# A fourth buffer for the high parts of expert weights, in place of one raw buffer

## The chip, the cores and the metric

The kernel runs on one core of one Trainium2 chip. The metric is the device time of one execution in microseconds (us). The median of three runs of the kernel before is 1669.49 us (1668.41 to 1675.79). A profiled execution took 1665.06 us; its span, from the first to the last instruction, is 1663.4 us.

## What is computed

A trunk of two layers works on 256 tokens of width 1024 in float32. Layer 0 is a mixer (gated positions and an attention with forgetting), a cross-attention to 256 memory tokens, and a dense SwiGLU of width 2816. Layer 1 is a second mixer (differential attention and a short convolution), another cross-attention, and a router that sends each token to 2 of 8 SwiGLU experts of width 3584. A norm ends it. This case is about the experts:

```python
def swiglu(h, wg, wu, wd):
    return (jax.nn.silu(h @ wg) * (h @ wu)) @ wd

def moe_swiglu(h, w_router, wg, wu, wd):
...
    logits = (t @ w_router).astype(jnp.float32)
    top_v, top_i = lax.top_k(logits, TOP_K)
    gates = jax.nn.softmax(top_v, axis=-1)
    combine = jnp.sum(jax.nn.one_hot(top_i, N_EXPERTS, dtype=jnp.float32) * gates[..., None], axis=1)
    for e in range(N_EXPERTS):
        out = out + combine[:, e:e + 1].astype(t.dtype) * swiglu(t, wg[e], wu[e], wd[e])
```

The three weight matrices of an expert are 1024 x 3584, 1024 x 3584 and 3584 x 1024 floats, 42 pieces of 1 MiB; the eight experts have 336.

## The kernel before

Every weight goes the same way, in pieces of 1 MiB (128 partitions x 2048 floats). A load on the sync engine's DMA queue (SP) brings it into a **raw** buffer. ACT copies it in two halves into a tile `wh` of a shorter float format (the high part, L121). DVE subtracts, `wl = raw - wh` (the low part, L123), and is the last to read the raw buffer. TensorE (PE) then multiplies: activations are split in the same way into `ch` and `cl`, or `hs` with its two halves, and a product is the sum of high x high (L138), low x high (L141) and high x low (L144). `mm3` issues the products with `wh` first, eight matmuls of a piece, and the four with `wl` behind them. So `wh` comes free earlier than `wl`. For the experts at the places 2, 4 and 7 (`SMALL`, at most 64 tokens) both parts of the activations stand side by side in the 128 columns, and `mm2` (L994) does with eight matmuls, four with `wh` and four with `wl`.

```python
    def pick(kind):
        lst = pools[kind]
        p = lst[cnt[kind] % len(lst)]
        cnt[kind] += 1
        return p
...
    def load_w(src, a, b, parts=1):
        r = load_raw(src, a, b, parts)
        p = pick("w")
        wh = p.tile([P, a, b], F32R, tag="wh", name="wh")
        wl = p.tile([P, a, b], F32R, tag="wl", name="wl")
```

Buffers come from pools in a fixed rotation. `wp` has three buffers for `wh` and three for `wl`. For the experts the raw rotation is written out as a list of eleven places (L1094): one of `rawp`, five that the earlier layers used for activations, `RAW2` = 3 of a pool `raw2`, one more of those activations (`V`), one of `rawp`. Each buffer is reused when its last reader is done; a load waits for that on the DMA queue.

An expert runs in four chunks of its 3584 columns (1024, 1024, 1024, 512). `gate_up` (L997) takes the chunk's pieces of the gate and the up matrix, `gated` (L1020) evicts the sums: on ACT `sg` (L1030, Silu; for the small experts `sgs`, L1026), on DVE the product (L1031). `to_hT` transposes on PE into `htp` and splits on ACT and DVE into `hs` (L129, L130). `down` (L1063) multiplies the chunk before by its down pieces into `y`. Once an expert, `slots_T` (`setp`, `st`), `gather_pair` (`xg`, `ch`), `slot_rstd` (`rsp`) and `scatter` (`y`, `sc`, `x`) stand between. All of these wait in the same in-order queues as the weight copies and subtractions. The order on each engine is made by the tile scheduler when the kernel is built, from the order of the code, the free buffers and the few `behind(...)` places that are written by hand; it is fixed in the program.

Before the last chunk of the last expert, `final_gain` (L1114) takes two places of the raw rotation: `gfrow`, read by two matmuls, and `gf`, the final norm's gain on all partitions, which is read by the last instructions of the program (`finish`, L1180).

```python
            p, tag = pick("raw")
            row = p.tile([1, D], F32, tag=tag, name="gfrow")
...
            p, tag = pick("raw")
            gf = p.tile([P, D], F32, tag=tag, name="gf")
```

Ten pieces follow it: four of gate and up, four down pieces of the chunk before, and two down pieces of the last chunk (L1202), which alone are loaded and split in two parts of 512 KB. Then `finish` scatters, norms and stores the output.

Of the kernel before, what the change touches and what calls it, by code (L numbers as in the profile page):

```python
# [12 lines left out]
F32R = mybir.dt.float32r  # L13
# [7 lines left out]
P = 128  # L21
# [6 lines left out]
DFF = 2816  # L28
DFFE = 3584
NE = 8  # L30
RAW2 = 3
WSPLIT = ((0, 0, 4), (1, 0, 4), (0, 4, 8), (1, 4, 8))
WSPLIT_MOE = ((0, 0, 4), (0, 4, 8), (1, 0, 8))
CHUNKS = ((0, 1024), (1024, 1024), (2048, 1024), (3072, 512))
# [21 lines left out]
def trunk_kernel(ctx: ExitStack, tc: tile.TileContext, io, out, stop=None):  # L56
# [6 lines left out]
    wp = ctx.enter_context(tc.tile_pool(name="wsplit", bufs=3))  # L63
# [17 lines left out]
    pools = {"raw": [(rawp, "raw")], "w": [wp], "split": WSPLIT}  # L81
# [12 lines left out]
# [6 lines that stand above are left out]
    def load_raw(src, a, b, parts=1):  # L100
        p, tag = pick("raw")
        r = p.tile([P, a, b], F32, tag=tag, name="raw")
        m = a // parts
        for i in range(parts):
            with behind(*gate):
                chain["dma"] = nc.sync.dma_start(r[:, i * m:(i + 1) * m, :], src[:, i * m:(i + 1) * m, :])
            gate.clear()
        return r

    def load_w(src, a, b, parts=1):  # L110
        r = load_raw(src, a, b, parts)
        p = pick("w")
        wh = p.tile([P, a, b], F32R, tag="wh", name="wh")
        wl = p.tile([P, a, b], F32R, tag="wl", name="wl")
        rf, hf, lf = (v.rearrange("p a b -> p (a b)") for v in (r, wh, wl))
        n = a * b // parts
        for part in range(parts):
            for i, c0, c1 in pools["split"]:
                sl = slice(part * n + c0 * n // 8, part * n + c1 * n // 8)
                if i == 0:  # L120
                    chain["wh"] = nc.scalar.activation(hf[:, sl], rf[:, sl], AF.Copy)  # L121
                elif i == 1:
                    chain["wl"] = nc.vector.tensor_sub(lf[:, sl], rf[:, sl], hf[:, sl].bitcast(F32))  # L123
                else:
                    nc.gpsimd.tensor_sub(lf[:, sl], rf[:, sl], hf[:, sl].bitcast(F32))
        return wh, wl
# [39 lines left out]
    def out_proj(cat, w, order, hook=None):  # L166
        ch, cl = cat
        acc = [[accp.tile([P, 512], F32, tag="acc", name="acc") for _ in range(2)] for _ in range(2)]
        def step(i, t, w2):
            wh, wl = w2  # L170
            for n in range(2):
                mm3([(acc[t][n], ch[:, order[i] * 2 + k, t * P:(t + 1) * P], cl[:, order[i] * 2 + k, t * P:(t + 1) * P],
                      wh[:, k, n * 512:(n + 1) * 512], wl[:, k, n * 512:(n + 1) * 512])
                     for k in range(2)], False, i == 0, i == 3)

        def piece(i):
            return load_w(w[order[i] * 256:(order[i] + 1) * 256, :].rearrange("(k p) n -> p k n", p=P), 2, D)

        for i in range(2):
            w2 = piece(i)  # L180
            for t in range(2):
                step(i, t, w2)
        last = [piece(2), piece(3)]
        for t in range(2):
            for i in range(2):
                step(2 + i, t, last[i])
            if hook is not None:
                hook(t, acc)
        return acc
# [50 lines left out]
    with ExitStack() as pre:  # L240
# [48 lines left out]
        def proj_ws(act, w, ncols, c0, into=None):  # L289

            ah, al = act
            wh, wl = load_w(w[:, c0:c0 + 256].rearrange("(k p) n -> p k n", p=P), KT, 256)
            ps = mmp.tile([P, 2, S], F32, tag="mm", name="pws") if into is None else into
            for f in range(2):
                o = ps[:, f, :]
                mm3([(o, wh[:, k, f * P:(f + 1) * P], wl[:, k, f * P:(f + 1) * P], ah[:, k, :], al[:, k, :])
                     for k in range(KT)], True, True, True)
            return ps

        def proj_ts(act, w, c0):  # L300

            ah, al = act
            pss = [accp.tile([P, 512], F32, tag="acc", name="pts") for _ in range(2)]
            for half in range(2):
                wh, wl = load_w(w[half * 512:(half + 1) * 512, c0:c0 + 512].rearrange("(k p) n -> p k n", p=P), 4, 512)
                for t in range(2):
                    mm3([(pss[t], ah[:, half * 4 + k, t * P:(t + 1) * P], al[:, half * 4 + k, t * P:(t + 1) * P],
                          wh[:, k, :], wl[:, k, :]) for k in range(4)], False, half == 0, half == 1)
            return pss
# [463 lines left out]
    with ExitStack() as moe:  # L773
        mA = moe.enter_context(tc.tile_pool(name="macts", bufs=1))
        sm = moe.enter_context(tc.tile_pool(name="msmall", bufs=2))
        m2 = moe.enter_context(tc.tile_pool(name="macts2", bufs=2))
        raw2 = moe.enter_context(tc.tile_pool(name="raw2", bufs=RAW2))

        def mbank(shape, name="mm"):
            return trp.tile(shape, F32, tag="tr", name=name)  # L780
# [311 lines left out]
        if done(4):  # L1092
            return
        pools["raw"] = ([(rawp, "raw")] + [(pA, tag) for tag in ("mh", "ml", "nh", "nl", "K")]  # L1094
                        + [(raw2, "raw")] * RAW2 + [(pA, "V"), (rawp, "raw")])
        cnt["raw"] = cnt["w"] = 0
        pools["split"] = WSPLIT_MOE
        xg_all = [catp.tile([P, 2, KT, P], F32R, tag=tg, name=tg) for tg in ("ch", "cl")]
        xg = xg_of(1)
# [209 lines left out]
```

## Time and profile before

| | |
|---|---|
| median of 3 runs | 1669.49 us (1668.41 to 1675.79) |
| profiled execution | 1665.06 us |
| its span, first to last instruction | 1663.4 us |
| mean granted TensorE clock | 0.992 of full speed |
| loads of expert weights | 112 + 112 + 110 of 1 MiB, 4 of 512 KB |
| HBM traffic | 461.90 MB read, 279 GB/s over the span |

In the profile, a group of instructions is named by its line, its engine and what it writes and reads (`wl<-raw,wh`); buffer numbers are left out. PE is the matmul engine, PEld its weight loads, SP the queue that issues the loads. A wait reads "who waited <- what ended the wait". The chain that ended last is followed back from the last instruction. The layers before the experts take the first 640 us or so; the experts run to about 1647 us.

### The profile page before, as it was taken

How to read it: one execution, taken by the hardware profiler on the slowest of the kernel's cores; microseconds unless marked ns; L12 is line 12 of the kernel's file. 1: busy time of each engine (PE TensorE's matmuls, PEld its weight loads, DVE VectorE, ACT ScalarE, POOL GpSimd, SP SyncE). 2: the span in 40 equal slices, each digit the busy share in tenths (PEclk: the TensorE clock that was granted, in tenths of full speed). 3: DMA queues.
4: the chain of work that ended last, by engine and by line, in shares of the span. 5: the costliest groups of instructions: out<-in, count | busy, mean ns of one | idle time of the engine just before them, and what ended most of it. 6: DMA issues, size and time to landing. Idle time of an engine off the chain costs nothing. (4 is left out here: it accounts for less than half of the span.)

```text
span 1663.4 us, 22408 instructions
## 1 busy us (share of the span) xinstructions
PE 1572.4 (95%) x8448; PEld 1310.2 (79%) x8448; DVE 1262.8 (76%) x1214; ACT 1074.4 (65%) x1396; POOL 47.1 (3%) x75
## 2 busy tenths in 40 slices
PE   8999999999999999999999889999889999999885
PEld 7799889999989887888887667777667777777653
DVE  6785655445576657899988988978888978988876
ACT  6555554344554446787777787767777767677775
POOL 1010010000000102000000000000000000000000
PEclk9999999999999999999999999999999999999998
DMA  7456466565535586899999999999999999999980
GB/s 237 163 178 214 145 217 201 177 200 180 191 127 178 187 333 245 322 341 354 360 369 361 345 358 339 338 338 375 345 363 345 340 337 347 329 351 345 358 309 28
DMA packets 175409, 464.50 MB, mean 279 GB/s; under 512 B 9074, under 2 KB 64390, under 8 KB 175164
## 3 DMA queue, kind: packets, MB, share of 16 engines
q1 hardware_dynamic: 174412, 459.80, 77.0%
q0 software_dynamic: 880, 3.19, 0.6%
q8 instruction: 68, 1.11, 0.3%
q14 instruction: 49, 0.40, 0.1%
HBM read 461.90 MB, written 2.11 MB: 279 GB/s over the span
## 5 line engine op out<-in xcount | busy, mean ns | idle before, releaser
L123 DVE TENSOR_TENSOR wl<-raw,wh 128x2048 fp32r<-128x2048 f32 (+1 forms) x527 | 983.0, 1894 | 238.0 <-ACT wh L121 235.7
L121 ACT ACTIVATE wh<-raw 128x1024 fp32r<-128x1024 f32 x866 | 852.7, 1049 | 277.1 <-PE pws L141 92.0
L138 PE MATMUL gu<-wh,ch 128*128 128x512 f32 x560 | 221.3, 396 | 2.8 <-ACT sg L1030 2.8
L141 PE MATMUL gu<-wh,cl 128*128 128x512 f32 x560 | 219.7, 393 | 0.0
L144 PE MATMUL gu<-wl,ch 128*128 128x512 f32 x560 | 152.8, 395 | 10.6 <-DVE wl L123 10.5
L138 PE MATMUL pws<-nh,wh 128*128 128x256 f32 x560 | 137.5, 283 | 0.0
L141 PE MATMUL pws<-nl,wh 128*128 128x256 f32 x560 | 137.4, 283 | 0.0
L144 PEld LDWEIGHTS gu<-wl,ch 128*128 128x128 f32 x560 | 103.5, 188 | 40.3 <-DVE wl L123 19.1
L138 PEld LDWEIGHTS gu<-wh,ch 128*128 128x128 f32 x560 | 105.5, 188 | 27.1 <-ACT sg L1030 2.9
L994 PE MATMUL gu<-wl,ch 128*128 128x512 f32 x336 | 99.8, 419 | 24.5 <-DVE wl L123 23.5
L141 PEld LDWEIGHTS gu<-wh,cl 128*128 128x128 f32 x560 | 105.6, 189 | 21.8 <-DVE cl L1111 0.4
L141 PE MATMUL y<-wh,hs 128*128 128x512 f32 x280 | 110.9, 396 | 0.0
L138 PE MATMUL y<-wh,hs 128*128 128x512 f32 x280 | 110.4, 394 | 0.0
L138 PEld LDWEIGHTS pws<-nh,wh 128*128 128x128 f32 x560 | 106.2, 190 | 1.3 <-ACT wh L121 0.9
L141 PEld LDWEIGHTS pws<-nl,wh 128*128 128x128 f32 x560 | 106.0, 189 | 0.4
L994 PEld LDWEIGHTS gu<-wl,ch 128*128 128x128 f32 x336 | 59.0, 191 | 55.1 <-DVE wl L123 45.9
L994 PE MATMUL gu<-wh,ch 128*128 128x512 f32 x336 | 97.7, 405 | 4.4 <-ACT wh L121 4.3
L138 PE MATMUL acc<-wh,ch 128*128 128x512 f32 x216 | 84.7, 392 | 0.0
L141 PE MATMUL acc<-wh,cl 128*128 128x512 f32 x216 | 84.4, 391 | 0.0
L994 PEld LDWEIGHTS gu<-wh,ch 128*128 128x128 f32 x336 | 63.3, 192 | 24.1 <-ACT wh L121 10.8
L144 PE MATMUL y<-wl,hs 128*128 128x512 f32 x280 | 79.1, 404 | 2.0 <-DVE wl L123 2.0
L144 PE MATMUL pws<-nh,wl 128*128 128x256 f32 x560 | 78.9, 283 | 0.0
(363 smaller groups left out, 2182.2 us busy)
## 6 DMA issues: line engine op xcount, KB each, us to landing
raw<-in_moe_w_up_dram SPq DMA_DIRECT2D x112, 1024.0 KB, 6.5
raw<-in_moe_w_gate_dram SPq DMA_DIRECT2D x112, 1024.0 KB, 6.4
raw<-in_moe_w_down_dram SPq DMA_DIRECT2D x110, 1024.0 KB, 6.2
raw<-in_mem_w_kv_dram SPq DMA_DIRECT2D x16, 1024.0 KB, 5.5
raw<-in_odd_w_in_dram SPq DMA_DIRECT2D x12, 1024.0 KB, 5.3
raw<-in_ffn_w_gate_dram SPq DMA_DIRECT2D x11, 1024.0 KB, 5.1
raw<-in_ffn_w_up_dram SPq DMA_DIRECT2D x11, 1024.0 KB, 5.2
raw<-in_ffn_w_down_dram SPq DMA_DIRECT2D x11, 1024.0 KB, 4.7
```

Of the source, the lines that this page charges most:

```text
L121: chain["wh"] = nc.scalar.activation(hf[:, sl], rf[:, sl], AF.Copy)
L123: chain["wl"] = nc.vector.tensor_sub(lf[:, sl], rf[:, sl], hf[:, sl].bitcast(F32))
L138: mm = nc.tensor.matmul(ps, ah, bh, start=f, stop=False, skip_group_check=bank)
L141: nc.tensor.matmul(ps, *((ah, bl) if w_left else (al, bh)), start=False, stop=False, skip_group_check=bank)
L144: mm = nc.tensor.matmul(ps, *((al, bh) if w_left else (ah, bl)), start=False, stop=e, skip_group_check=bank)
L994: mm = nc.tensor.matmul(ps, a, b[which], start=f, stop=e)
```

## The change

The list of pools for the split pieces gets a fourth entry, a new pool `wp2` of one buffer, for `wh` alone: every fourth `wh` lies there. `wl` always comes from `wp` and keeps its three buffers. The memory, 8 KiB a partition, is that of one `raw2` buffer: `RAW2` is 2, and the raw rotation has ten places. The layers before the experts are as they were.

```diff
-RAW2 = 3
+RAW2 = 2
...
         wh = p.tile([P, a, b], F32R, tag="wh", name="wh")
-        wl = p.tile([P, a, b], F32R, tag="wl", name="wl")
+        wl = wp.tile([P, a, b], F32R, tag="wl", name="wl")
...
         raw2 = moe.enter_context(tc.tile_pool(name="raw2", bufs=RAW2))
+        wp2 = moe.enter_context(tc.tile_pool(name="wsplit2", bufs=1))
...
         cnt["raw"] = cnt["w"] = 0
+        pools["w"] = [wp] * 3 + [wp2]
         pools["split"] = WSPLIT_MOE
```

The scheduler's order changes in places. The first is ACT, expert 0, where the first evictions `sg` and the first `hs` stand. Before:

```order
L121 ACTIVATE wh_6325<-raw_6323 128x1024 x2
L121 ACTIVATE wh_6344<-raw_6342 128x1024 x2
L1030 ACT_TABLE_LOAD
L1030 ACTIVATE sg_6279<-gu_6136,rs_6277 128x512
L1030 ACTIVATE sg_6279<-gu_6137,rs_6277 128x512
L129 ACTIVATE hs_6286<-htp_6287 128x512
L129 ACTIVATE hs_6294<-htp_6295 128x512
L121 ACTIVATE wh_6363<-raw_6361 128x1024 x2
```

Now, with all numbers three higher and lines from L778 on one or two further:

```order
L121 ACTIVATE wh_6328<-raw_6326 128x1024 x2
L121 ACTIVATE wh_6347<-raw_6345 128x1024 x2
L121 ACTIVATE wh_6366<-raw_6364 128x1024 x2
L1031 ACT_TABLE_LOAD
L1031 ACTIVATE sg_6282<-gu_6139,rs_6280 128x512
L1031 ACTIVATE sg_6282<-gu_6140,rs_6280 128x512
L129 ACTIVATE hs_6289<-htp_6290 128x512
L129 ACTIVATE hs_6297<-htp_6298 128x512
```

The copies of one more piece (6363, now 6366) stand ahead of `sg` and `hs`. About ten groups of `sg`, `hs` and `ch` in experts 0 and 1 have moved so by one piece on ACT, with their partners on DVE. From the second pieces of expert 2 on, ACT, DVE and PE have the same order in both kernels, but for a few matmuls of the last piece.

The second place is the DMA queue, at the loads behind `final_gain` (the names in brackets are the engines or DMA lanes whose semaphore a load waits for). Before, the last six rows of loads:

```order
L106 DMA raw_13424<-in_moe_w_down_dram 128x2x1024 [waits DMAHW2_49,DVE_49]
L106 DMA raw_13439<-in_moe_w_down_dram 128x2x1024 [waits DMAHW3_49,DVE_49]
L106 DMA raw_13469<-in_moe_w_down_dram 128x1024 [waits DMAHW4_49,DVE_49]
L106 DMA raw_13469<-in_moe_w_down_dram 128x1024 [waits DMAHW5_49]
L106 DMA raw_13480<-in_moe_w_down_dram 128x1024 [waits DMAHW6_49,PE_49]
L106 DMA raw_13480<-in_moe_w_down_dram 128x1024 [waits DMAHW7_49]
```

Now:

```order
L106 DMA raw_13427<-in_moe_w_down_dram 128x2x1024 [waits DMAHW2_49,DVE_49]
L106 DMA raw_13442<-in_moe_w_down_dram 128x2x1024 [waits DMAHW3_49,DVE_49]
L106 DMA raw_13472<-in_moe_w_down_dram 128x1024 [waits DMAHW4_49,PE_49]
L106 DMA raw_13472<-in_moe_w_down_dram 128x1024 [waits DMAHW5_49]
L106 DMA raw_13483<-in_moe_w_down_dram 128x1024 [waits DMAHW5_49,DMAHW6_49,DMAHW4_49,DVE_49]
L106 DMA raw_13483<-in_moe_w_down_dram 128x1024 [waits DMAHW7_49]
```

Order and kind of the loads are the same. The wait for PE (the matmuls that read `gfrow`) has moved from the last piece to the one before it, and the last piece (13483) waits for the lanes 4 and 5, which load the piece before it (13472), and for DVE: both have the same place in `raw2`, since `gf` keeps the other.

## Rows read from the trace of the kernel before

**Rows 1.** The page: busy time (share) and instructions; DMA busy tenths in 40 slices.

```profile
PE 1572.4 (95%) x8448; PEld 1310.2 (79%) x8448; DVE 1262.8 (76%) x1214; ACT 1074.4 (65%) x1396; POOL 47.1 (3%) x75
DMA  7456466565535586899999999999999999999980
```

**Rows 2.** Stretches: length, busy PE PEld DVE ACT POOL, clock, DMA share, GB/s.

```profile
643.00:884.00 241.00, 238.15 (x1086) 196.24 (x1085) 216.91 (x191) 187.39 (x209) 0.00 (x0) 0.99 0.94 351
884.00:1642.00 758.00, 695.57 (x3124) 535.86 (x3122) 640.75 (x451) 561.04 (x675) 0.00 (x0) 1.00 0.92 336
```

**Rows 3.** Waits of PE, 643 to 884 us: total us, times, longest us.

```profile
PE gu L138 <- ACT sg L1030: 2.8, 1, 2.8
```

**Rows 4.** Tile raw, 884 to 1590 us, and the DMA queue's waits in it.

```profile
L123 DVE TENSOR_TENSOR wl<-raw,wh x234: 2277/2284/2294, 884.4 to 1588.0; 128x2048 fp32r<-128x2048 f32 x117
DMA to landing us min/median/max: 4.7/6.5/8.5
...
SPq L106 <- DVE wl L123: 457.4, 194, 5.6
```

**Rows 5.** Waits of ACT, 643 to 884 us; then timeline rows of ACT and PE there.

```profile
ACT wh L121 <- PE gu L141: 25.7, 39, 0.8
ACT wh L121 <- PE y L141: 15.8, 20, 1.2
...
654.77 2.01 ACT L121 ACTIVATE wh<-raw 128x1024 fp32r<-128x1024 f32 x2 [0.71 <-PE gu L141]
...
660.22 2.00 ACT L121 ACTIVATE wh<-raw 128x1024 fp32r<-128x1024 f32 x2 [0.71 <-PE gu L141]
...
766.79 1.07 PE L144 MATMUL gu<-wl,ch 128*128 128x512 f32 x4
```

**Rows 6.** Waits of ACT, DVE and PE, 884 to 1642 us.

```profile
ACT hs L129 <- PE y L144: 51.8, 14, 5.9
ACT wh L121 <- PE gu L141: 4.3, 7, 0.7
...
DVE wl L123 <- ACT wh L121: 80.4, 67, 3.9
...
PE gu L994 <- DVE wl L123: 23.5, 33, 1.6
PE y L994 <- DVE wl L123: 17.2, 24, 1.4
PE gu L144 <- DVE wl L123: 10.5, 19, 0.9
```

**Rows 7.** Timeline of ACT and DVE in expert 3: start us, us, what [idle before].

```profile
1084.88 0.38 ACT L979 ACTIVATE st<-setp 128x256 fp32r<-128x256 f32 x1 [3.82 <-PE setp L977]
...
1087.77 2.29 DVE L123 TENSOR_TENSOR wl<-raw,wh 128x2048 fp32r<-128x2048 f32 x1 [3.46 <-ACT wh L121]
```

**Rows 8.** The DMA queue at the start of the experts: a wait, and an issue.

```profile
SPq L106 <- PE rlp L812: 13.3, 1, 13.3
...
633.28 0.37 SPq L106 DMA_DIRECT2D raw<-in_moe_w_gate_dram  x1
```

**Rows 9.** Tile raw, 1613 to 1617 us, then 1600 to 1664 us.

```profile
L106 SPq DMA_DIRECT2D raw<-in_moe_w_down_dram x4: 333/339/355, 1613.9 to 1615.6; - x4
...
DMA to landing us min/median/max: 4.9/6.1/7.4
...
L121 ACT ACTIVATE wh<-raw x31: 614/1044/1067, 1599.9 to 1643.1; 128x1024 fp32r<-128x1024 f32 x23, 128x512 fp32r<-128x512 f32 x8
L123 DVE TENSOR_TENSOR wl<-raw,wh x17: 1216/2285/2293, 1599.4 to 1645.2; 128x2048 fp32r<-128x2048 f32 x13, 128x1024 fp32r<-128x1024 f32 x4
```

**Rows 10.** The chain that ended last, from 1636 us: start us, us, what.

```profile
1642.94 3.50 DVE wl L123 x3
...
1646.48 0.51 PE y L994
```

**Rows 11.** DMA issues: count, KB each, median us to landing.

```profile
x<-in_x_dram SPq DMA_DIRECT2D x2, 512.0 KB, 3.4
```

## The prediction

> **What bounds the kernel now.** I read the page first. Engine shares over the whole span tell little here, so note only that no engine is full [rows 1]: PE 95% by a busy time that counts pipelined matmuls, DVE 76%, ACT 65%, and that the DMA digits stand at 9 from the 18th slice on. From there the experts run.
>
> The stretches split the expert stage in two [rows 2]. 643 to 884 us holds experts 0 and 1, 884 to 1642 us the other six, after that comes the end. In the first stretch PE is busy 238.15 of 241 us and its only wait on another engine is 2.8 us, once [rows 3]: PE is the bound. In the second PE has 695.57 of 758 us, DVE 640.75, ACT 561.04: none is full, they hold each other up.
>
> Loads look like the limit (DMA share 0.92) but are not. 234 splits from 884.4 to 1588.0 us make 703.6 / 233 = 3.02 us a tile, and a load lands 4.7 to 8.5 us after its issue [rows 4]. The DMA queue waits 457.4 us, 194 times, for a `wl` subtraction, the last reader of a raw buffer [rows 4]: loads are late because buffers are full, not the reverse. Eleven buffers turn over in 11 x 3.02 = 33 us; less 8.5 us to land and some 9 us of splitting (two copies 2.1, one subtraction 2.3, with waits of up to 3.9 each [rows 6] counted in), a landed tile lies unused for at least 15 us.
>
> Next the waits, by stretch. Before 884 us ACT waits for PE to give back a `wh` buffer: 25.7 + 15.8 us in 59 waits [rows 5]. That is the wait the fourth buffer removes, and it stands where PE is the bound. After 884 us the same wait is 4.3 us in 7 cases. What stops ACT there is its own order: `hs`, `sgs`, `sg`, `st` and `y` stand in its queue and need a PE result, 51.8 us for `hs` alone. DVE then waits 80.4 us for `wh`, and PE 23.5 + 17.2 + 10.5 = 51.2 us for `wl` [rows 6]. One such case: at 1084.88 us ACT has idled 3.82 us for `setp`, and DVE's next subtraction idles 3.46 us behind it [rows 7].
>
> **The change, part by part.**
>
> *The fourth `wh` buffer, experts 0 and 1.* ACT starts a tile when PE has ended the high products of the third tile before; the rows repeat 2.01 us of copies after 0.71 us of waiting, 2.72 us a tile, which is PE's own pace [rows 5]. With four buffers ACT starts one tile sooner, and PE is no faster: 0 us. What DVE can gain is its lead at 884 us. Before, its subtraction begins 2.0 us (two copies) after PE ended those products; in the changed kernel it is held by the three `wl` buffers, which PE gives back four matmuls, 1.07 us, after them [rows 5]. So DVE enters expert 2 up to 1.0 us earlier. I take **-1.0 us**, since DVE limits expert 2; the bounds are 0 and, with all of the 4.3 us as well, -5.3 us.
>
> *The fourth `wh` buffer, experts 2 to 7.* The order listings of both kernels are the same on ACT, DVE and PE from early in expert 2 almost to the end; the sequence around `setp` [rows 7] stands unchanged. So ACT meets the same PE results at the same places, with fewer than three tiles in hand, and the buffer stays unused: 0 us of the 80.4.
>
> *The moved rows on ACT.* In experts 0 and 1 about ten `sg`, `hs` or `ch` groups stand one tile of copies (2.0 us) later. At the first, the copies from 660.22 us started when a buffer came free [rows 5], and `sg` stands right behind them. Now there is one buffer more: the same instant starts the copies of the next tile, `sg` stands behind these, and begins when it did: 0 us. If the cover fails, see rival 2.
>
> *One raw buffer less.* The ring shrinks by 3.0 us out of at least 15: 0 us. At the start of the stage four loads of chunk 1 change places on the DMA queue; the load that waits 13.3 us for the router's matmuls and is issued at 633.28 us is now the first of that chunk, lands by 633.3 + 8.5 = 642 us, and its copies start at 654.77 us [rows 5, 8]: 0 us.
>
> *The last load.* This is what costs. `final_gain` draws two raw buffers; its `gf` stays in one until the end. Both now come from the two-buffer pool, and so do the last two tiles. The last tile must therefore share a buffer with the one before it: in the listing its DMA waited for PE and now waits for that tile's loads and DVE. In the trace of before it is issued at about 1615.1 and 1615.6 us and is there long before its turn [rows 9]. In the changed kernel it goes out when the preceding tile's second `wl` ends. The last three of the chain's `wl` run 3.50 us from 1642.94; the first of them is that one, so it ends at 1642.94 + 3.50 / 3 = 1644.1, and the third at 1646.44 [rows 10]. The halves go out at 1644.15 and, by the spacing (1615.6 - 1613.9) / 3 = 0.57, 1644.7. How long the second takes alone is not shown: the four of its size took 4.9 to 7.4 us among others [rows 9], the quietest of 512 KB 3.4 us [rows 11]. I take 4.3, between 3.4 and 4.9, as little else moves then: 1649.0. Then two copies of 0.61 and a subtraction of 1.22 [rows 9], 2.4 us: 1651.4, against 1646.4. **+5.0 us**, bounds +4.1 (3.4 us) and +8.1 (7.4 us). Nobody hides it: that `wl` chain is the chain that ended last [rows 10], PE needs the tile for both halves of `y`, and behind it on DVE stand only `y` and what follows; on the DMA queue only the output.
>
> **Sum**: -1.0 + 5.0 = +4.0 us on the profiled execution's 1665.06, so 1669.1. That execution is 4.4 us under the median shown, 1669.49; I forecast against the median: **1673.5 us**. 0.5% is 8.3 us, about what a measurement of this kernel can tell from no change.
>
> **The rivals.**
>
> 1. *The bubbles close* (faster). The same gap stands again and again on DVE before `wl`: 80.4 us in 67 waits. If it stood for a missing buffer, a fourth could take what PE loses to it, 51.2 us; half of that, with the end's cost, gives 1669.5 - 26 + 5 = 1648. Against it: 4.3 us of buffer waits and the unchanged order. The Trainium skill's Perfetto Trace Analysis, Optimization Strategy, says that a gap repeating on an engine that should be saturated can mean that memory for the next tile ran out; the trace does not bear it out here after 884 us, and does before it, on an engine that is not the bound. Chance 0.07.
>
> 2. *The moved rows come late* (slower). If ACT has not gained a tile where `sg` or `hs` was put behind one more, PE waits 2.0 us longer for its banks or its `hs`, at ten places: up to 20 us, 1669.5 + 4 + 20 = 1693. It shows as a loss over 0.5% from three such places on (4 + 3 x 2 = 10 > 8.3). For it: PE's one wait there, 2.8 us for `sg`, is of this kind. Against it: 41.5 us of ACT's idle time there were buffer waits. Chance 0.07.
>
> 3. *The last load does not matter* (the change does nothing at the end): the wait is over early, or a shorter queue elsewhere pays for it. Then 1669.5 - 1.0 = 1668.5. Against it: the subtraction waited for is itself on the last chain. Chance 0.13.
>
> **How the numbers follow.** The forecast has 0.73. Of it 0.70 is within 0.5% and 0.03 above, for the 8.1 us bound with a slow landing. Faster by over 0.5%: 0.07, rival 1. Slower: 0.07 + 0.03 = 0.10. Within: 0.70 + 0.13 = 0.83. The range takes rival 3 and the bounds: low end 1669.5 - 5.3 + 4.1 = 1668.3, and 2 us less since the runs shown start 1.1 below their median, 1666; high end 1669.5 + 8.1 = 1677.6, and as much again, 1679. Outside lie rival 1 and most of rival 2.
>
> **What would show it.** From 884 us to about 1638, less about 1 us, all as before: DVE still waits some 80 us for `wh`, ACT some 50 us for `hs`. ACT's waits on PE for `wh` before 884 us gone. The DMA queue's last two loads not at 1615 us but some 28 us later, right behind a `wl`; then an idle DVE of about 6 us on the chain that ended last. Loads still landing in 5 to 8 us. The prediction is wrong if DVE's wait for `wh` shrinks by tens of us (rival 1), if PE waits for `sg` or `hs` before 884 us (rival 2), or if the final `wl` follows its forerunner without a gap (rival 3).

## The result, and the profile after

The changed kernel took 1679.23 us, median of 13 runs (1673.82 to 1684.78), against 1669.36 us for the kernel before in the same session (13 runs, 1663.7 to 1675.79). The ratio is 1.0058, 95% interval [1.0041, 1.0075]. Run again in another session (the experiment after_again) it took 1675.29 us against 1668.1, ratio 1.0045 [1.0032, 1.0057]. So the change costs 7 to 10 us, about half a per cent; forecast were +4.0 us, and the first median lies 0.23 us above the top of the range.

The page, busy time by engine and DMA tenths, against [rows 1]: the same numbers of instructions, PE busy 11 us longer.

```profile
PE 1583.6 (94%) x8448; PEld 1315.4 (78%) x8448; DVE 1264.0 (75%) x1214; ACT 1072.2 (64%) x1396; POOL 47.0 (3%) x75
...
DMA  7456456555545586899999999999999999999971
```

The stretches of the expert stage, the border shifted by 7 us since the layers before came out later (columns as in [rows 2]). In a stretch of the same length as before, 758 us, PE, DVE and ACT do the same work in the six later experts, at the same rate of loads.

```profile
643.00:891.00 248.00, 245.11 (x1118) 201.28 (x1118) 222.49 (x196) 189.03 (x211) 6.71 (x4) 0.99 0.94 346
891.00:1649.00 758.00, 696.04 (x3122) 535.01 (x3121) 638.37 (x449) 557.91 (x671) 0.00 (x0) 1.00 0.92 337
```

The waits of 650 to 891 us, the same work as 643 to 884 us before [rows 3, 5]. PE's one wait for `sg` is 2.9 us, before 2.8. ACT's waits for a `wh` buffer have shrunk only from 41.5 to 37.2 us, and DVE now waits for its three `wl` buffers (11.1 us).

```profile
ACT wh L121 <- PE gu L141: 22.5, 33, 1.7
ACT wh L121 <- PE y L141: 14.7, 18, 1.3
DVE wl L123 <- PE gu L144: 11.1, 23, 1.2
...
PE gu L138 <- ACT sg L1031: 2.9, 1, 2.9
```

The waits of 891 to 1649 us, the same work as 884 to 1642 us before [rows 6]. Of ACT's waits for a `wh` buffer, 4.3 us before, none is listed any more; the waits behind them are about what they were: DVE 79.6 us for `wh` (80.4 before), PE 24.6 + 15.9 + 10.2 = 50.7 us for `wl` (51.2 before).

```profile
DVE wl L123 <- ACT wh L121: 79.6, 65, 4.0
ACT hs L129 <- PE y L144: 55.3, 14, 6.5
...
PE gu L995 <- DVE wl L123: 24.6, 36, 1.6
...
PE y L995 <- DVE wl L123: 15.9, 23, 1.4
PE gu L144 <- DVE wl L123: 10.2, 19, 0.9
```

**Where the time went.** I took the end of the subtraction of the same piece (on DVE) in both traces, and how the difference to the kernel before grows from piece to piece. Experts 0 and 1 are the pieces 1 to 84; 335 and 336 are the two split pieces at the end. The table has every profile of this study, in us; the columns add up to the difference of the spans, but for rounding.

| kernel | to piece 1 | 1 to 73 | 73 to 85 | 85 to 90 | 90 to 334 | to the last wl | the end | sum |
|---|---|---|---|---|---|---|---|---|
| changed | +6.8 | -0.1 | +2.9 | -0.9 | +1.5 | +4.7 | +1.0 | +16.0 |
| after_again | +0.8 | +0.3 | +2.9 | -0.9 | +3.4 | +4.7 | +1.0 | +12.2 |
| tail_free | +2.8 | -0.3 | +2.9 | -0.9 | +1.5 | 0 | +0.4 | +6.5 |
| ring10 | +2.2 | +2.5 | +1.8 | -0.9 | +0.2 | +4.7 | +0.9 | +11.6 |
| handover | +3.4 | -0.3 | 0 | +1.3 | +1.5 | 0 | +0.8 | +6.8 |
| late_fourth | +2.8 | -0.2 | +1.8 | -0.9 | +1.4 | 0 | -0.2 | +4.7 |
| last_shared | +0.8 | +2.6 | 0 | 0 | +1.4 | +4.6 | +0.4 | +9.8 |
| ring10_tail | +5.9 | -0.1 | +1.8 | -0.9 | -0.8 | 0 | +0.1 | +6.0 |
| ahead3 | +2.3 | -0.1 | 0 | 0 | -19.9 | 0 | +0.8 | -16.8 |
| ahead_r10 | +0.5 | -1.0 | +1.8 | -0.9 | -19.5 | 0 | +0.8 | -18.2 |
| ahead4 | +3.9 | -0.3 | +2.9 | -0.9 | -18.5 | 0 | +0.3 | -12.6 |
| ahead3_3 | +0.9 | -0.1 | -0.1 | 0 | -20.2 | 0 | 0 | -19.5 |
| ahead4_3 | +8.8 | -0.1 | +2.9 | -0.9 | -18.1 | 0 | +0.7 | -6.7 |

Three columns carry the change: the two from piece 73 to 90, where expert 1 hands over to expert 2, and the last load. The first column and, in the first eight rows, the columns "1 to 73" and "90 to 334" (single steps of 0.4 to 1.6 us) follow the granted clock, which differs from execution to execution (last section).

**The handover.** In all of ACT's order, the kernel with the shorter ring alone (ring10_tail) differs from the kernel before in one row, the `hs` of the last chunk of expert 1, which stands one piece of copies *earlier*. The changed kernel has the same row there:

```
-L121 ACTIVATE wh<-raw 128x1024 x12
-L129 ACTIVATE hs<-htp 128x512
-L121 ACTIVATE wh<-raw 128x1024 x4
+L121 ACTIVATE wh<-raw 128x1024 x10
+L129 ACTIVATE hs<-htp 128x512
+L121 ACTIVATE wh<-raw 128x1024 x6
```

The timeline of ACT there, kernel before (start, us, what, [idle before]): `hs` follows the copies without a gap.

```profile
882.39 2.01 ACT L121 ACTIVATE wh<-raw 128x1024 fp32r<-128x1024 f32 x2 [0.79 <-PE y L141]
884.31 0.58 ACT L129 ACTIVATE hs<-htp 128x512 fp32r<-128x512 f32 x1
```

The same in ring10_tail, three `wh` buffers and the row moved: ACT stops 2.15 us in front of `hs`.

```profile
885.31 2.01 ACT L121 ACTIVATE wh<-raw 128x1024 fp32r<-128x1024 f32 x2 [0.79 <-PE y L141]
889.48 0.60 ACT L129 ACTIVATE hs<-htp 128x512 fp32r<-128x512 f32 x1 [2.15 <-PE htp L1057]
```

And ACT and DVE in the changed kernel, the row moved and four buffers:

```profile
884.58 2.01 ACT L121 ACTIVATE wh<-raw 128x1024 fp32r<-128x1024 f32 x2 [0.77 <-PE y L141]
891.54 0.60 ACT L129 ACTIVATE hs<-htp 128x512 fp32r<-128x512 f32 x1 [4.95 <-PE htp L1058]
...
892.17 0.69 DVE L130 TENSOR_TENSOR hs<-htp,hs 128x512 fp32r<-128x512 f32 x1 [1.51 <-ACT hs L129]
894.07 6.70 DVE L123 TENSOR_TENSOR wl<-raw,wh 128x2048 fp32r<-128x2048 f32 x3 [1.20 <-DMA raw<-in_moe_w_gate_dram]
```

ACT is one piece further ahead, 2.80 us at this pace (0.79 of waiting and 2.01 of copies), and waits 4.95 = 2.15 + 2.80 us for the same transposes of PE. Behind them DVE, which PE waits for in expert 2, idles 1.51 + 1.20 us. (The second gap is put down to a load; it ends when ACT's next copies do, 892.04 + 2.0.) Expert 2 gets its first piece 2.9 us later and wins back 0.9.

These are times of DVE. PE, the bound in experts 0 and 1, splits the loss another way. How much later than in the kernel before PE begins its first expert matmul and the first of expert 2 (883.48 us before, 891.26 in the changed kernel), and how much later piece 90 is split, in us (kernels whose low clock stands at the same places of experts 0 and 1 as before):

| kernel | PE, first of the experts | PE, first of expert 2 | piece 90 |
|---|---|---|---|
| changed | 6.78 | 7.79 | 8.78 |
| tail_free | 2.62 | 3.59 | 4.59 |
| handover | 3.27 | 4.21 | 4.48 |
| late_fourth | 2.67 | 2.51 | 3.50 |
| ring10_tail | 5.80 | 5.72 | 6.71 |

From PE's first matmul of expert 2 to piece 90 the moved row costs 1.0 us with four buffers and with three alike; only handover, which puts it back, loses 0.3. The other 1.0 us PE has lost before, in experts 0 and 1, and only where the fourth buffer is used there. It goes piece by piece. These are PE's matmuls with `wl`, the last of a piece, in three pieces one after another in the changed kernel, and in the first two of the same pieces in late_fourth, which uses three buffers there:

```profile
799.78 1.08 PE L144 MATMUL gu<-wl,ch 128*128 128x512 f32 x4
802.57 1.09 PE L144 MATMUL gu<-wl,ch 128*128 128x512 f32 x4
805.30 1.07 PE L144 MATMUL gu<-wl,ch 128*128 128x512 f32 x4
```

```profile
794.95 1.08 PE L144 MATMUL gu<-wl,ch 128*128 128x512 f32 x4
797.68 1.07 PE L144 MATMUL gu<-wl,ch 128*128 128x512 f32 x4
```

In the changed kernel the second piece takes 2.79 us and the third 2.73, in late_fourth the second 2.73. The second is a fourth piece of the rotation. All 14 gate and up pieces of experts 0 and 1 that stand at a fourth place take about 0.07 us longer in every kernel that uses the buffer there, together 1.0 us, and none does in the others. So PE reads a `wh` in the fourth buffer a little slower; why was not found.

**The last load.** The chain that ended last in the changed kernel, against [rows 10]:

```profile
1652.08 2.36 DVE wl L123 x2
1654.46 3.24 DMA raw<-in_moe_w_down_dram
...
1657.79 0.64 ACT wh L121
...
1658.47 3.87 PE y L995 x7
```

And the timeline of its DMA queue, where the last two loads of [rows 9] stood at about 1615 us:

```profile
1654.46 0.86 SPq L106 DMA_DIRECT2D raw<-in_moe_w_down_dram  x2
```

Both halves go out as the `wl` of the piece before ends, and the copies start 3.33 us later. A load stands on the chain where there was none. From the `wl` of the 334th piece to the last instruction it is 1679.4 - 1652.2 = 27.2 us, before 1663.4 - 1641.9 = 21.5: +5.7 us. Of it 4.7 stand before the last `wl`. Counted from there, the last multiplication of the output comes 0.7 us later than before (0.4 to 0.8 in the four profiles in which the last two pieces share a buffer, 0.0 in all others). The rest of the column "the end" is the store of the output, 7.8 to 8.9 us in these profiles, with and without the late load.

### The profile page after: what moved, and what is told of

It reads as the page before. It is cut to its first block, busy times and chain, and to the rows that moved or that the text cites. A ratio compares the mean times of both kernels' runs of the same rounds, so it can differ in the third digit from the quotient of the medians.

```text
span 1679.4 us, 22409 instructions
## 1 busy us (share of the span) xinstructions
PE 1583.6 (94%) x8448; PEld 1315.4 (78%) x8448; DVE 1264.0 (75%) x1214; ACT 1072.2 (64%) x1396; POOL 47.0 (3%) x75
## 5 line engine op out<-in xcount | busy, mean ns | idle before, releaser
L144 PE MATMUL gu<-wl,ch 128*128 128x512 f32 x560 | 153.6, 395 | 10.2 <-DVE wl L123 10.2
L995 PE MATMUL gu<-wl,ch 128*128 128x512 f32 x336 | 99.4, 418 | 25.6 <-DVE wl L123 24.6
```

Source lines behind the costliest of these rows:

```text
L144: mm = nc.tensor.matmul(ps, *((al, bh) if w_left else (ah, bl)), start=False, stop=e, skip_group_check=bank)
L995: mm = nc.tensor.matmul(ps, a, b[which], start=f, stop=e)
```

## The experiments

Theory: the last load costs 5 to 6 us, the handover 1 to 2 us, and the fourth buffer gives nothing, since what ACT waits for is set by its order. Rivals: the shorter ring starves the loads; the fourth buffer itself is at fault; the loss before the experts belongs to the kernel.

### tail_free: the last piece in a buffer of its own

```diff
-            w2 = [down_piece(pe, pc, i, 2) for i in range(2)]
+            w2 = [down_piece(pe, pc, 0, 2)]
+            cnt["raw"] = 9
+            w2.append(down_piece(pe, pc, 1, 2))
```

Made on the changed kernel. Expected:

> The changed kernel, with the last piece loaded into a buffer of rawp instead of the raw2 buffer of the piece before it; nothing else moves but a few matmuls of that piece. Theory (the shorter raw ring costs twice, at the last load and at one moved row between experts 1 and 2; the fourth wh buffer does nothing): the last two loads go out some 28 us before they are needed, the final subtractions follow each other without a gap, the end after the piece before the last is 5.7 us shorter than in the changed kernel, and the time is about 2.3 us above the kernel before (1.0014). Rival (the fourth buffer's moved rows in experts 0 and 1, or something else, made the loss): the time stays 8 to 10 us above before.

Measured: 1672.0 us, ratio 1.0016 [0.9997, 1.0035], against 1668.21 for the kernel before in this batch. The column of the last load is 0. The columns of the handover remain.

### ring10: ten raw buffers, no fourth buffer

```diff
-RAW2 = 3
+RAW2 = 2
```

Made on the kernel before, nothing else. Expected:

> The kernel before with RAW2 = 2 alone: ten raw buffers, three wh buffers. Theory: as slow as the changed kernel, 8 to 9 us above before (1.005), with the last load waiting for the subtraction before it (+5.7 us) and ACT's hs of the last chunk of expert 1 standing one piece earlier, which DVE pays with about 2 us before its second subtraction of expert 2. Rival (the fourth buffer costs): the last load's 5.7 us alone, and DVE reaches expert 2 as in the kernel before.

Measured: 1674.74 us, ratio 1.0031 [1.0011, 1.005], less than the 8 to 9 us expected. The last load costs 4.7 us, the handover 1.8 - 0.9. These costs come with the shorter ring; the fourth buffer is not needed for them. By the traces what it lacks against the changed kernel is the 1.0 us that PE loses there in experts 0 and 1.

### handover: the moved row put back

```diff
-                hT = to_hT(e, sg, ((mA, "hs"), (pA, "gain")))
+                if (e, c) == (1, nch - 1):
+                    e2, c2 = divmod(e * nch + c + 1, nch)
+                    ready = [gate_piece(wg, e2, c2, i) for i in range(3)]
+                    with behind("wh"):
+                        hT = to_hT(e, sg, ((mA, "hs"), (pA, "gain")))
+                else:
+                    hT = to_hT(e, sg, ((mA, "hs"), (pA, "gain")))
```

On tail_free; the next `gate_up` takes the pieces in `ready`. Expected:

> The kernel tail_free with one row put back: the hs split of the last chunk of expert 1 stands behind the copies and the subtraction of the third piece of expert 2, as in the kernel before. Theory: the 2.0 to 2.9 us that DVE lost there go away, and of the forecast gain of 1.0 us for the lead something shows: 0 to 1 us under before (0.9994 to 1.0). Rival (the lead over PE is lost to the three wl buffers, not to the row): DVE still arrives about 2 us late and the time is that of tail_free, 1.0014.

Measured: 1670.21 us, ratio 1.0009 [0.9991, 1.0026]; in the total it can't be told from the kernel before, nor from tail_free. The 2.9 us at piece 85 are gone, but 1.3 us come back by piece 90. So the row explains the gap at 891 us. Counted from PE's first matmul of expert 2, putting it back brings the loss from 1.0 down to 0.3 us. What comes back is mostly PE's own delay: it begins expert 2 late by 0.9 us that it has lost in experts 0 and 1, and ACT waits 2.72 us for the first `sgs` there, in the kernel before 1.93. The expected gain from a lead of DVE did not show.

### late_fourth: the fourth buffer from expert 2 on only

On tail_free: `pools["w"]` keeps its three entries at first, and

```diff
+            if e == 2:
+                pools["w"], cnt["w"] = [wp] * 3 + [wp2], 0
```

Expected:

> The kernel tail_free with the fourth wh buffer used from expert 2 on only; experts 0 and 1 rotate over three, in the order of before but for the hs row between experts 1 and 2. Theory (the buffer is unused from expert 2 on): from expert 2 to the end the pieces take the time of before within 1 us, the loss is the moved row's, 2 to 3 us (1.0015). Rival (the fourth buffer helps where DVE waits): experts 2 to 7 shorter by more than 5 us, the time under before.

Measured: 1670.74 us, ratio 1.0018 [1.0002, 1.0034]. By the trace the handover costs 1.8 - 0.9 us, as with three buffers, and the experts 2 to 7 as before but for a step of 1.1 us at 1619 us with 10.2 us at the low clock, where the kernel before has 3.4. With the fourth buffer in the experts 0 and 1 too (tail_free) the columns say 2.9 - 0.9. The 1.1 us more are PE's 14 slower pieces, which late_fourth does not have, and not the handover: from PE's first matmul of expert 2 to piece 90 both lose 1.0 us. The medians, 1670.7 and 1672.0, agree in sign but can't tell 1 us apart.

### after_again: the changed kernel once more

No edit. Expected:

> The changed kernel once more, nothing edited, on the chip of the runs of this batch. Open is whether the +6.7 us up to the 24th weight tile (about 100 us), which went with 6.8 us at half granted clock at 46 to 57 us, belongs to the kernel or to the execution: the code there is the same. Theory 'execution': the low stretch is one that comes and goes; this profile may have 0 to 7 us more than the before up to tile 24 (2 us or so where a single stretch of 6.8 us stands there), and the difference of the medians stays at the sum of handover and last load, +6.5 to +9 us. Rival 'kernel': the same two stretches of low clock (6.8 us each) and the same +6.7 us stand in this profile too, and the difference of the medians is +10 us or more, as in the first comparison (1679.23 against 1669.36).

Measured: 1675.29 us, ratio 1.0045 [1.0032, 1.0057], profile 1677.35. To the first piece +0.8 us instead of +6.8, handover and last load as in the first profile. The loss before the experts belongs to the execution.

### last_shared: only the last load, on the kernel before

```diff
-            w2 = [down_piece(pe, pc, i, 2) for i in range(2)]
+            w2 = []
+            for i in range(2):
+                cnt["raw"] = 1
+                w2.append(down_piece(pe, pc, i, 2))
```

Eleven raw buffers; both split pieces draw the same one. Expected:

> The kernel before (eleven raw buffers, three wh) with one edit: the last two pieces are both put into one raw buffer, so the last load waits for the piece before it, as in the changed kernel. It isolates the last load. Theory: the last load's term is worth 5.0 to 5.7 us by itself, the time is 1668.4 + 5.5 = 1674 us and the ratio 1.003; the last issue stands right behind the wl of the piece before, the halves land after 3.2 to 3.6 us, nothing before 1630 us differs. Rival 'it is mostly the clock after PE has idled' : the piece-to-end distance grows by more than 6.5 us. Rival 'ring': the cost needs the shorter ring as well, then this kernel is within 2 us of the before.

Measured: ratio 1.0036 [1.0015, 1.0057], that is +6.0 us (interval 2.5 to 9.5). Its chain that ended last has the same load in the same place:

```profile
1646.57 2.37 DVE wl L123 x2
...
1648.96 3.14 DMA raw<-in_moe_w_down_dram
...
1652.20 0.64 ACT wh L121
```

The handover is 0 here. The trace gives 4.6 us for the last load and 0.7 behind it, up to the store of the output; 1.4 + 2.6 us of this profile's other columns go with the low clock.

### ring10_tail: only the shorter ring

```diff
-RAW2 = 3
+RAW2 = 2
...
-            w2 = [down_piece(pe, pc, i, 2) for i in range(2)]
+            w2 = [down_piece(pe, pc, 0, 2)]
+            cnt["raw"] = 9
+            w2.append(down_piece(pe, pc, 1, 2))
```

Made on the kernel before. Expected:

> Ten raw buffers, three wh buffers, and the last piece moved to a buffer of its own (the place of rawp), so the only thing left of the change is the shorter ring. Theory 'the shorter ring moves a row': the cost at the handover from expert 1 to expert 2 (hs one piece earlier on ACT and DVE) is there without the fourth wh buffer, +1 to +2 us, and the last load costs 0: 1668.4 + 1.5 = 1670 us, ratio 1.001. Rival 'the shorter ring starves the loads': loss of several us spread over experts 2 to 7, 1673 us or more. Rival 'the fourth buffer does it': no loss at the handover, 1668.4 us.

Measured: 1669.18 us, ratio 1.0005 [0.9993, 1.0016]. The moved row's 1.0 us are there in the trace (1.8 - 0.9 in the table), the last load costs nothing, and the loads aren't starved. In the total so little can't be told from 0.

### ahead3: another order, no change of buffers

```diff
-                hT = to_hT(e, sg, ((mA, "hs"), (pA, "gain")))
+                if 2 <= e and (e, c) != (NE - 1, nch - 1):
+                    e2, c2 = divmod(e * nch + c + 1, nch)
+                    ready = [gate_piece(wg, e2, c2, i) for i in range(2)]
+                    with behind("wh"):
+                        hT = to_hT(e, sg, ((mA, "hs"), (pA, "gain")))
+                else:
+                    hT = to_hT(e, sg, ((mA, "hs"), (pA, "gain")))
```

On the kernel before, with `ready` passed to the next `gate_up`. From expert 2 on, the copies of the next chunk's first two gate pieces stand ahead of `hs` and `hsm`. Expected:

> The kernel before (eleven raw, three wh) with another order from expert 2 on: the first two gate pieces of the next chunk are made before the transposes and hs of the chunk before, and hs and hsm stand behind their copies, so ACT has two tiles more in hand when it stops for a PE result. Theory 'the order makes the bubbles, not the buffers': DVE's 80 us of waits for wh from 884 us on shrink by some 10 to 40 us and PE's 51 us of waits for wl with them; 1645 to 1663 us with only three wh buffers. Rival 'buffers': with three wh buffers ACT waits for PE to give one back as soon as it is ahead (waits of ACT for gu L141 and y grow from 4 us to 20 us or more) and the time stays within 3 us of 1668.4 or gets worse, and it would take the fourth buffer to go below. Rival 'hs comes late': PE waits for hs before its down products, time over 1672 us.

Measured: 1648.96 us, ratio 0.9894 [0.9872, 0.9916], faster than the kernel before by over 1% (19 us), with the same three `wh` and eleven raw buffers. The waits of ahead3 in 886 to 1624 us, the same work as 884 to 1642 us before [rows 6]:

```profile
ACT wh L121 <- PE y L141: 20.8, 22, 1.7
ACT hs L129 <- DVE hsm L1050: 19.2, 18, 2.7
...
ACT hs L129 <- PE y L144: 10.2, 6, 1.7
...
PE gu L994 <- DVE wl L123: 18.6, 36, 1.6
PE y L994 <- DVE wl L123: 10.6, 11, 1.4
PE gu L144 <- DVE wl L123: 8.0, 14, 0.8
```

ACT stops 10.2 us for `hs` behind `y` instead of 51.8. Its waits in front of `hs` of every kind fall from 84.8 to 32.9 us, though 19.2 of these, for DVE's `hsm`, are mostly new (1.9 before). PE's waits for `wl` shrink from 51.2 to 37.2 us, and all of its listed waits for other engines from 61.0 to 44.2: 16.8 us of the 19.9 in the column "90 to 334". The rest was not assigned to rows.

### ahead_r10 and ahead4: the fourth buffer under the new order

ahead_r10 has ahead3's order and ring10_tail's edits. ahead4 adds the change's fourth `wh` buffer to it:

```diff
+        wp2 = moe.enter_context(tc.tile_pool(name="wsplit2", bufs=1))
...
+        pools["w"] = [wp] * 3 + [wp2]
```

Expected:

> The order of ahead3 with ten raw buffers, three wh buffers and the last piece in a buffer of its own: the control for the next kernel. Theory 'the ring has slack': the shorter ring costs only what it cost without the new order, about 1 us at the handover; 1649 + 1 = 1650 us. Rival 'with the faster order the ring is short': loads now run at 356 GB/s with a DMA share of 0.96 over 852 to 1600 us, so waits of DVE or ACT on the loads appear, 1653 us or more.

> The same with the fourth wh buffer, so the only difference from ahead_r10 is the edit of the change. Theory 'the order decides whether the buffer is used': in ahead3 ACT waited 32 us (21.6 + 5.4 + 5.1) after 884 us for PE to give back a wh buffer, which is what a fourth buffer removes; some of it reaches PE, so this kernel is 2 to 10 us faster than ahead_r10, 1640 to 1648 us, and ACT's waits for wh on PE fall below 10 us. Rival 'the fourth buffer is worth nothing here either': within 1.5 us of ahead_r10, since ACT then waits as long for the next PE result. Rival 'the loads are the bound now': the same time and waits of DVE and ACT on DMA.

Measured: 1648.36 us, ratio 0.9882 [0.9856, 0.9909], and 1652.04 us, ratio 0.9905 [0.9881, 0.9929]. The expected gain of 2 to 10 us did not come; the fourth buffer's kernel has the higher median, with intervals that overlap. The waits of ahead_r10, 885 to 1623 us:

```profile
ACT wh L121 <- PE y L141: 20.7, 22, 1.7
...
ACT hs L129 <- PE y L144: 10.2, 6, 1.7
...
ACT wh L121 <- PE gu L141: 5.4, 8, 0.8
ACT wh L121 <- PE htp L1057: 5.1, 3, 1.7
ACT hs L129 <- PE htp L1057: 2.1, 1, 2.1
...
PE gu L994 <- DVE wl L123: 18.6, 35, 1.6
PE y L994 <- DVE wl L123: 11.9, 12, 1.4
PE gu L144 <- DVE wl L123: 8.0, 14, 0.8
```

And those of ahead4, 890 to 1629 us, the same work:

```profile
ACT hs L129 <- PE y L144: 30.3, 6, 5.4
...
ACT wh L121 <- PE y L141: 7.1, 8, 1.1
...
ACT hs L129 <- PE htp L1058: 2.5, 1, 2.5
...
ACT wh L121 <- PE gu L141: 0.8, 1, 0.8
...
PE gu L995 <- DVE wl L123: 19.2, 37, 1.6
PE y L995 <- DVE wl L123: 10.7, 11, 1.4
PE gu L144 <- DVE wl L123: 7.9, 14, 0.8
```

The buffer is used here: ACT's waits for `wh` fall from 20.7 + 5.4 + 5.1 = 31.2 to 7.9 us. But its waits on PE for `hs` in these rows rise from 12.3 to 32.8 us, and PE's for `wl` stay at 38 us. The wait has moved to the next row in ACT's queue that needs PE. The medians are 3.7 us apart. The traces show 1.1 us more between piece 73 and 90, PE's slower pieces of experts 0 and 1, and 1.0 us in the experts 2 to 7, whose source was not sought; another 4 us between these two profiles arise before piece 73, with the clock.

### ahead3_3 and ahead4_3: three pieces ahead

As ahead3 and ahead4, with

```diff
-                    ready = [gate_piece(wg, e2, c2, i) for i in range(2)]
+                    ready = [gate_piece(wg, e2, c2, i) for i in range(2 if c2 == nch - 1 else 3)]
```

Expected:

> As ahead3 (eleven raw, three wh), but three gate pieces instead of two stand ahead of the transposes in the wide chunks. Theory: with three wh buffers the third piece can only be copied once PE has used up the first of the three, so ACT cannot be a tile further ahead; 0 to 5 us slower or faster than ahead3 (1649). Rival 'more is better': 1645 us or less without the fourth buffer. Rival 'hs late': hs stands so late that PE waits for it, over 1655 us.

> As ahead3_3, with ten raw buffers, four wh buffers and the last piece in a buffer of its own. Theory 'the order decides': the fourth buffer is worth more where three pieces stand ahead, so it is faster than ahead3_3 by 2 to 10 us and the fastest of all kernels here, 1636 to 1646 us. Rival 'worth nothing': within 1.5 us of ahead3_3 plus the 1 us of the shorter ring.

Measured: 1646.9 us, ratio 0.9871 [0.9849, 0.9894], and 1654.63 us, ratio 0.9911 [0.9886, 0.9935]. Again four buffers are not better than three: -18.1 against -20.2 us in the experts 2 to 7 from piece 90 on. Here they are worse: the fastest of the six runs with four, 1651.01 us, is slower than the slowest of the six with three, 1648.1. (ahead4_3 also has one raw buffer less and with it the moved row, 1.0 us. 7.9 us of the difference of these two profiles arise before the experts, with the clock, but that profile is the slowest of its six runs.) ahead3_3 has the lowest median of all; from ahead3 and ahead_r10 it can't be told apart.

## Why the prediction was off

It said +4.0 us by a sum of -1.0 and +5.0. The causes that the traces show make 1.0 (PE's slower pieces) + 1.0 (the moved row) + 4.7 (the last load) + 0.4 to 0.8 (behind it) = 7.1 to 7.5 us. The second comparison has +7.2 us; the first has over 2 us more, and its interval, 6.8 to 12.5 us, holds the sum.

**The fourth buffer, experts 0 and 1: -1.0 us. This step failed**, in sign: with the fourth buffer PE loses 1.0 us in experts 0 and 1 instead. The step took PE, the bound there, as neither faster nor slower, and the lead of DVE as worth something in expert 2. But PE takes 0.07 us longer over each of the 14 gate and up pieces whose `wh` lies in the fourth buffer. The lead came, as PE's delay: DVE ends its last subtraction of expert 1 at 890.66 us instead of 883.92, 6.7 us later, and PE begins expert 2 7.8 us later. It was worth nothing, since `hs` stands in both queues before expert 2 and waits for PE; with the row put back (handover) no gain came either. The bounds, 0 to -5.3 us, had no loss in them; "nothing or a gain" was assumed, not read.

**The moved rows: 0 us.** Failed too: they cost 1.0 us. That PE's wait for `sg` stays (2.9 us), and that the rows which moved one piece later cost nothing, was borne out: PE's 14 slower pieces account for what it lost before expert 2. But one group had moved one piece *earlier*, and that is the one that costs: 1.0 us from PE's first matmul of expert 2 to piece 90 in each profile that has it, with three buffers and with four; 0 without it, and 0.3 with it put back by hand. The text spoke of groups moved by one piece with their partners and gave all of them the same sign.

**One raw buffer less: 0 us.** Right for the loads, 4.7 to 8.9 us to landing in the changed kernel, and ring10_tail's total. Wrong in that the shorter ring moves the row: the order is made from the free buffers, so no edit of a pool is without effect on the queues until the rows are compared one by one.

**The fourth buffer, experts 2 to 7: 0 us.** Right. From piece 90 to 334 the changed kernel takes 1.5 us more, a step at some 1009 us that stands with 3.4 us at the low clock in this execution; last_shared, with three buffers, has the same step, and ring10 and ring10_tail have neither. The buffer can be there or not without effect that the trace shows (late_fourth, ring10_tail).

**ACT's waits for `wh` before 884 us gone.** Wrong: 37.2 us are left of 41.5. ACT comes one piece further and then waits for the fourth buffer as it had for the third, since PE is slower than it.

**The last load: +5.0 us.** Right in mechanism and place. From the forerunner's `wl` to the last `wl` the forecast was 1651.4 - 1644.1 = 7.3 us, measured 1661.4 - 1654.4 = 7.0. Two errors in it cancel by luck: the first copy starts 3.3 us after that `wl`, where 4.9 us were given to the second half's landing, and the splitting took 1657.79 to 1661.43 = 3.6 us, not 2.4, because both halves' four copies then stand in a row. Not in the sum was what comes behind: 0.4 to 0.8 us on PE at the low clock. With it the last load costs 5.0 to 5.5 us by the traces; last_shared's total is 6.0.

**Rival 1, the bubbles close**, fell twice: here, and under an order where the buffer is used (ahead4). A part of the bubbles was ACT's order: moving `hs` behind two more pieces took 19 us out of the kernel without a buffer. The Trainium skill's Perfetto Trace Analysis, Optimization Strategy, says that a repeating gap can mean too few buffers; for this gap that did not hold. **Rival 2** was seen in its form (ACT late at `hs`), but once, not ten times, and on a row that moved the other way. **Rival 3** is refuted by last_shared.

## What to carry to other kernels

A buffer helps an in-order engine only as far as the next row in its queue that waits for someone else: look there first, and move that row before buying memory; here that was worth 19 us, and the memory nothing. Ask of a new buffer too whether its reader takes as long over it as over the others; here the reader, the bound, did not. When a rotation gets shorter, compare the queues row by row with the sign of each move, and ask which two tiles at the end of the program now share a place, since nothing hides a load there. Give a term a loss as its bound unless a row excludes one.

## What the runs showed of the hardware

The clock before the experts comes and goes. In 40 to 70 us, code that no edit here touches, the stretches of the changed kernel's first profile and of after_again read (columns as above, the granted clock third from the end):

```profile
40.00:70.00 30.00, 28.59 (x105) 20.54 (x105) 18.67 (x33) 13.86 (x31) 0.00 (x0) 0.77 0.39 123
```

```profile
40.00:70.00 30.00, 29.12 (x152) 22.36 (x151) 23.82 (x43) 16.28 (x35) 0.00 (x0) 1.00 0.51 158
```

PE is busy in both, at 2.4 GHz throughout in the second and at 1.2 GHz for part of the stretch in the first. By the first expert piece that is +6.8 and +0.8 us; the first is more than any term of the prediction. Nine of the thirteen other profiles lie 2 us or more behind the one of the kernel before at that point. What sets it in an execution was not found; with one profile of each kernel, their spans can't be compared.

The wait for the last load slows what follows. In 1655 to 1664 us of the changed kernel PE has waited for it, and the granted clock is 0.64 (the lower level for most of the stretch); in the same part of the kernel before, which has no wait, it is 1.00:

```profile
1655.00:1664.00 9.00, 5.56 (x12) 3.00 (x11) 3.46 (x4) 3.39 (x6) 0.00 (x0) 0.64 0.32 117
```

```profile
1640.00:1650.00 10.00, 7.48 (x28) 4.56 (x27) 8.78 (x9) 5.10 (x11) 0.10 (x1) 1.00 0.00 0
```

The late transfer thus costs its own length and then 0.4 to 0.8 us more, from the last `wl` to the last multiplication of the output, in the four profiles that have it. The Trainium skill's TensorE: Matmul & The Clock Gate, HAM oscillation, describes PE falling back to the low clock in waits for loads; this trace agrees at this place.

Behind a pair of 512 KB loads with nothing else in flight the copies start 3.2 to 3.3 us after the first issue (1654.46 to 1657.79, and in last_shared 1648.96 to 1652.20), below the 4.9 us that the fastest of the four took among other loads [rows 9].

A matmul's pace can hang on the buffer that it reads. In experts 0 and 1 a gate or up piece takes PE 2.79 us where its `wh` lies in the fourth buffer and 2.73 elsewhere, with the granted clock at 1.00 (2.4 GHz) in both places (799 to 808 us in the changed kernel, 794 to 803 us in late_fourth). The down pieces show no such loss. Whether the place in memory or something else sets it was not tried.
